# Second layer's latents: the spread of the keys' root and the key scale's product move inside the second query latent's section

## The chip, the cores and the metric

The kernel runs on one core of a Trainium2 chip. The time is device time in microseconds, the median of several executions. Lower is better. Five queues work at once on the core: PE (TensorE, matmuls and transposes, its weight loads shown apart as PEld), DVE (VectorE), ACT (ScalarE), POOL (GpSimd, which here mostly issues DMAs) and SP (SyncE, DMAs only). Each takes its instructions in the order in which the program was written, and waits on semaphores for the others.

## The reference

A two-layer encoder trunk: sequence 1024, width 1024, all in float32. Each layer has a mixer (latent attention beside a convolution branch) and a gated feed-forward part. The change is in the mixer's projections, of which this is what matters:

```python
h = _rmsnorm(x, g_mix[l])
p = h @ w_in[l]
c_q = _rmsnorm(p[..., :384], g_q[l])                  # query latent, 3 blocks of 128 channels
q = (c_q @ w_uq[l]).reshape(b, s, 8, 64 + 32)
c_kv = _rmsnorm(p[..., 384:640], g_kv[l])             # key/value latent, 2 blocks of 128
kv = (c_kv @ w_ukv[l]).reshape(b, s, 8, 64 + 64)      # k_nope and v
k_rope = _apply_rope(p[..., 640:672], cos, sin)
...                                                   # softmax attention over 8 heads
u = a * jax.nn.sigmoid(gt)                            # a, gt: the other 1024 columns of p
u = _dwconv(u, w_dw_conv[l], b_dw_conv[l])            # 31 taps along the sequence
```

## The kernel before

Activations lie transposed: 128 channels on the partitions, the 1024 tokens along the free dimension. A projection of 128 output channels is one **section** of PE work. A float32 product is made of three products of split operands (high and low parts, names ending in `h` and `l`), so a section of the second layer has 8 blocks of input channels x 3 products x 2 halves of 512 tokens = 48 matmuls.

The method `project` writes one layer's sections in a fixed order (`seq`). The part of the second layer that matters is: `kv0`, `kv1` (key/value latents), `kr` (the shared rotary key), `q0`, `q1`, `q2` (query latents), then `k0` to `k3` (keys, from the normalised `kv` latents), `u0`, `u1` (rotary parts of the queries) and `n0` to `n3` (the rest of the queries), both from the query latents. After each section's matmuls the loop calls `work`, which writes out what other engines have to do by then: each piece of follow-up work is a generator whose steps give an estimate of DVE time and of a delay, and `work` takes whichever step is due by a modelled clock, filling with convolution taps (`conv`, DVE) where nothing is due. So DVE and ACT instructions stand in the order in which `work`, `emit`, `after` and `evict` wrote them, and nothing is reordered when it runs.

What follows a latent section: ACT copies it out of PSUM (`cq<-pq`), squares it (`qss<-cq`), and makes its high part (`cqs_0h`), DVE the low part (`cqs_0l`) and the sum of squares. The keys' norm works like this:

- After `q0`'s matmuls PE transposes the summed squares (`rkv1t`), DVE reduces them and takes the root (`rkv1v`, `rkv1q`, `rkv1y`, function `roots`).
- `keys_norm`: PE spreads the root over the partitions by 8 transposes (`rkv1s`, function `spread`), ACT copies the two halves into `rkv`, DVE multiplies both latents by it (`ckv<-ckv,rkv`), ACT makes `kvs_0h` and `kvs_1h`, DVE `kvs_0l` and `kvs_1l`. The `k` sections read these four.
- `key_scale`: one small PE product (`kt`) sums numbers over the partitions, seven small DVE instructions make a power of two from it (`qk`), and the rotary key is split with it (`krs`, ACT then DVE).

PSUM in this stage: three full-width buffers (two banks each), taken in turn by the sections, and two single banks, taken in turn by `rkv1t`, `rkv1s` and `kt`. With the turn shift that stands before `q2`, `k0` takes the buffer of `q1`, `k2` that of `q2`, `k3` that of `k0`, `u0` that of `k1`. A `k` section's buffer comes free when DVE has made the low part of `ks` from it, after ACT has made the high part. `kt` takes the bank of the first half of `rkv1s`, so it waits for ACT's first copy into `rkv`.

Beside this ACT does work for later: `far` (a tap of the convolution scaled on ACT and added by an accumulating DMA that POOL issues), `wor` (sums of squares of the output weights), and `wu21l`, `wu01l`, `wu11l` (the negated high parts of weights; the load of the high part, `wu11h` and so on, is a DMA that POOL issues, in POOL's order behind the DMAs of the `far` tiles).

After `k3`, PE transposes the sum of the queries' squares (`rq1t`), `u0` runs, and PE spreads the queries' root (`rq1s`) between `u0` and `u1`; from there on the rest of the queries hangs.

Of the kernel before, what the change touches and what calls it, by code (L numbers as in the profile page):

```python
# [95 lines left out]
HALVES = (slice(0, 512), slice(512, T))  # L96
# [50 lines left out]
class Encoder:  # L147
# [102 lines left out]
                                           op0=ALU.mult, op1=ALU.subtract)  # L250
        return hi, lo

    def product(self, ps, weights, moving, by_half=False):
        nc = self.nc
        n = len(moving)
        for halves in ((0,), (1,)) if by_half else ((0, 1),):
            for k in range(n):
                (wh, wl), (xh, xl) = weights(k), moving[k]
                rest = ((wl, xh), (wh, xl)) if n <= 3 else ((wh, xl), (wl, xh))
                for s, (w, x) in enumerate(((wh, xh), *rest)):  # L260
                    for c in halves:
                        nc.tensor.matmul(ps[:, HALVES[c]], w, x[:, HALVES[c]], start=(k == 0 and s == 0),  # L262
                                         stop=(k == n - 1 and s == 2))
# [324 lines left out]
    def project(self, l, carry):  # L588
        nc, a = self.nc, self.a
        par = self.par[l]  # L590
        clock = {"pe": 0.0, "dve": 0.0}
        taps, active, u, conv, away, far_at = [], [], {}, {}, {}, {}
        gates, ckv, kvs, cq, cqs, vs, w = {}, [], [], [], [], [], {}
# [29 lines left out]
        def key_scale():  # L623
            sums = self.bank(f"kt{l}", (128, 3))
            nc.tensor.matmul(sums, self.ones, col(4, 3), start=True, stop=True)
            nc.vector.tensor_copy(out=col(4, 3), in_=sums)
            nc.vector.scalar_tensor_tensor(out=col(4), in0=col(4), scalar=float(KVL), in1=col(5), op0=ALU.mult, op1=ALU.mult)
            nc.vector.tensor_tensor(out=col(4), in0=col(4), in1=col(6), op=ALU.add)
            self.half_exponent(col(5), col(4))
            self.power(col(6), col(5), -1.0, 200.0)  # L630
            self.power(col(2), col(5), 1.0, 54.0)
            nc.vector.tensor_scalar(out=col(2), in0=col(2), scalar1=SCALE, scalar2=None, op0=ALU.mult)
            launch(key_rope_end())

        def work(until):
            while True:
                at = next((e for e in active if e[0] <= clock["dve"]), None)
                if at is None and taps and clock["dve"] + TAP <= until:
                    j, t = taps.pop(0)
                    self.conv_step(l, j, u[j], conv[j], t)  # L640
                    clock["dve"] += TAP
                    continue
                if at is None:
                    at = min(active, key=lambda e: e[0], default=None)
                    if at is None or at[0] > until:
                        return
                    clock["dve"] = max(clock["dve"], at[0])
                step = next(at[1], None)
                if step is None:
                    active.remove(at)  # L650
                else:
                    clock["dve"] += step[0]
                    at[0] = clock["dve"] + step[1]

        def launch(steps, n=-1):
            active.append([clock["pe"], steps, n])
# [5 lines left out]
                    e[0] = clock["dve"] + step[1]  # L662
                active.remove(e)

        def start(steps):
            next(steps)
            active.append([clock["pe"] + 1.8, steps, 99])

        def gate(j):
            g = gates[j] = self.blk(f"gate{l}_{j}")  # L670
# [52 lines left out]

        def keys_norm():
            r = st["rkv"] = self.blk(f"rkv{l}")
            for s, p in zip(HALVES, self.spread(rooted("kroot"), f"rkv{l}", HALVES, self.bank)):
                nc.scalar.copy(out=r[:, s], in_=p)
            yield 0.0, 1.8
            for j in range(2):
                nc.vector.tensor_tensor(out=ckv[j], in0=ckv[j], in1=r, op=ALU.mult)  # L730
                yield 1.25, 0.0
            both = [parts(ckv[j], f"kvs{l}_{j}", kvs, par[:, P_GKV + j:P_GKV + j + 1]) for j in range(2)]
            yield [next(p) for p in both][0]
            for p in both:
                yield from p
# [34 lines left out]
        def key_rope_end():  # L770
            t, hl = st.pop("kr"), self.blk(f"krs{l}", F16, (128, 2, T))[0:32]
            by = qk[0:32, 6:7]
            nc.scalar.activation(out=hl[:, 0], in_=t, func=AF.Copy, scale=by)
            yield 0.0, 1.5
            nc.vector.scalar_tensor_tensor(out=hl[:, 1], in0=t, scalar=by, in1=hl[:, 0], op0=ALU.mult, op1=ALU.subtract)
            self.move(krd, hl)
            yield 1.25, 0.0

        def query_latent(j):
            yield from latent(f"q{j}", cq, "qss", j)  # L780
            yield from parts(cq[j], f"cqs{l}_{j}", cqs, par[:, P_GQ + j:P_GQ + j + 1])

        def parts(src, name, out, scale):
            hi, lo = self.blk(name + "h", F32R), self.blk(name + "l", F32R)
            nc.scalar.activation(out=hi, in_=src, func=AF.Copy, scale=scale)
            yield 0.0, 1.5
            nc.vector.scalar_tensor_tensor(out=lo, in0=src, scalar=scale, in1=hi.bitcast(F32),
                                           op0=ALU.mult, op1=ALU.subtract)
            out.append((hi, lo))
            yield 1.25, 0.0  # L790
# [61 lines left out]

        def inputs(name):
            if l:
                return lambda: self.product(ps[name], lambda k: (w[name][:, 0, k], w[name][:, 1, k]), hl)
            return lambda: self.product(ps[name], self.tiled(w[name]), hl)

        def ranked(group, j, n, name, moving):
# [15 lines left out]
        def rooted(out):  # L874
            e = pending.pop(out)
            if e in active:
                for step in e[1]:
                    clock["dve"] = max(clock["dve"], e[0]) + step[0]
                active.remove(e)
            return st.pop(out)  # L880

        seq = []
        add = lambda name, weight, emit, evict, after=None: seq.append((name, weight, emit, evict, after))
# [10 lines left out]
            add(f"kv{j}", f"kv{j}", inputs(f"kv{j}"), lambda j=j: latent(f"kv{j}", ckv, "kss", j))  # L894
        add("kr", "kr", shared_key, key_rope)
        add("q0", "q0", inputs("q0"), lambda: query_latent(0), lambda: root("kss", "kroot", KVL, "rkv"))
        add("q1", "q1", inputs("q1"), lambda: query_latent(1), lambda: (start(keys_norm()), key_scale()))
        add("q2", "q2", inputs("q2"), lambda: query_latent(2))
        between = {2 + l: lambda: root("qss", "qroot", QL, "rq")}
        norm = lambda: start(queries_norm())  # L900
# [36 lines left out]
        hl, rx, ps = self.first_sections(l, supply) if l == 0 else self.next_sections(l, carry, supply)  # L937
# [295 lines left out]
    def up_steps(self, l, steps, put):  # L1233
# [238 lines left out]
        for q, (i, f) in enumerate(seq):  # L1472
            n = base + q
            steps.append(lambda i=i, f=f: product(i, f))
            m = EVICT.get((i, f), n + 1)
            put(int(m), m % 1 * 10, lambda i=i, f=f: evict(i, f))
# [844 lines left out]
```

## Time and profile before

| | |
|---|---|
| runs | 2175.66 us median of 3 (2175.47 to 2175.92) |
| profiled execution | 2174.71 us, of which the instructions' span is 2172.9 us |
| PE busy | 2160.1 us, 99% of the span |
| DVE, ACT, POOL busy | 1859.4 us (86%), 1480.1 us (68%), 517.2 us (24%) |
| granted TensorE clock, mean | 0.999 of 2.4 GHz |

The busy shares are means over the whole kernel. PE's share leaves 12.8 us of the span in which it isn't busy; whether an edit can win or lose time is seen from where PE waits, and for whom.

### The profile page before, as it was taken

Reading aid. Unit: us, or ns where it says so; the run is one execution under the profiler, and the core shown is the slowest. Engines: PE = TensorE matmul, PEld = TensorE weight load, DVE = VectorE, ACT = ScalarE, POOL = GpSimd, SP = SyncE. Lnnn points to the kernel's source line nnn. Section 1 sums busy time; section 2 is a strip of 40 time slices with the busy share of each in tenths; the row PEclk is TensorE's granted clock in tenths of the full one; section 3 lists DMA queues with packets and bytes.
Section 4 is the critical chain, followed back from the end, with each engine's and each line's share of the span. In section 5 each row is a group of like instructions: output and inputs, shape, how many; then the busy total and the mean of one; then the engine's idle time right before and its main releaser. Section 6 shows DMA issues by size and latency. Waiting matters only on the chain.

```text
span 2172.9 us, 29815 instructions
## 1 busy us (share of the span) xinstructions
PE 2160.1 (99%) x10726; PEld 1178.3 (54%) x10726; DVE 1859.4 (86%) x2558; ACT 1480.1 (68%) x2208; POOL 517.2 (24%) x506
## 2 busy tenths in 40 slices
PE   9999999999999999999999999999999999999998
PEld 8887666754444444444444576667544444444445
DVE  6989999879998887887978889998898988878877
ACT  6365888746898889554533768886478888865544
POOL 1232767211211111000000356771111111110000
PEclk9999999999999999999999999999999999999999
DMA  6898878854689898555334986786646988856533
GB/s 193 180 192 209 169 147 167 257 150 117 140 238 260 225 286 264 191 173 186 115 121 101 201 209 137 157 196 192 174 102 161 264 242 242 238 140 218 191 114 121
DMA packets 161220, 400.95 MB, mean 185 GB/s; under 512 B 19840, under 2 KB 27888, under 8 KB 161072
## 3 DMA queue, kind: packets, MB, share of 16 engines
q1 hardware_dynamic: 104080, 266.79, 35.8%
q0 software_dynamic: 56704, 131.74, 33.7%
q8 instruction: 84, 1.38, 0.3%
q10 hardware_dynamic: 288, 0.53, 0.1%
q14 instruction: 64, 0.52, 0.1%
HBM read 270.75 MB, written 69.66 MB: 157 GB/s over the span
## 4 chain that ended last, share of the span: by engine, by line
PE 93%; DVE 3%; ACT 2%; DMA 1%; issue 1%; DVEq 0%; SPq 0%; ACTq 0%
PE p L1376 36%; PE pd L1650 18%; PE po L1082 7%; PE s L1935 7%; PE t L1975 5%; PE pa L262 3%; PE o L1997 2%; PE pg L262 2%; PE pn L262 2%; PE pq L262 2%; PE pkv L262 1%; PE o L2002 1%; PE pg L585 1%; PE pv L1911 1%; PE pk L262 1%; DVE conv L2156 1%
## 5 line engine op out<-in xcount | busy, mean ns | idle before, releaser
L1376 PE MATMUL p<-b,w 128*128 128x512 f16 x3696 | 800.3, 379 | 0.3
L1376 PEld LDWEIGHTS <-w 128*128 128x128 f16 x3696 | 358.8, 98 | 431.7 <-issue 1.0
L1650 PE MATMUL pd<-ab,wd 128*128 128x512 f16 (+1 forms) x1920 | 401.0, 371 | 0.4 <-DVE ab L1640 0.4
L1252 POOL DMA_DIRECT2D wu<-in_w_up x176 | 152.5, 880 | 770.3 <-DVE w L1340 582.2
L1650 PEld LDWEIGHTS <-wd 128*128 128x128 f16 x1920 | 187.9, 98 | 210.7 <-issue 0.9
L1935 PE MATMUL s<-k,q 96*128 96x512 f16 x768 | 186.9, 379 | 0.0
L1340 DVE SCALAR_TENSOR_TENSOR w<-wu,wf,w 128x512 f16<-128x512 f32 (+1 forms) x216 | 177.3, 835 | 5.7 <-ACT w L1337 5.7
L1978 DVE SCALAR_TENSOR_TENSOR pt<-t,pt 128x512 f16<-128x512 f32 x256 | 163.0, 677 | 10.0 <-ACT pt L1977 9.0
L1337 ACT ACTIVATE w<-wu,wf 128x512 f16<-128x512 f32 (+1 forms) x216 | 165.2, 783 | 0.4 <-DMA wu<-in_w_up 0.4
L1977 ACT ACTIVATE pt<-t 128x512 f16<-128x512 f32 x256 | 139.2, 596 | 32.0 <-PE t L1975 30.0
L1937 DVE TENSOR_REDUCE mx<-s 128x1 f32<-128x1024 f32 x128 | 155.0, 1211 | 1.0 <-PE s L1935 1.0
L1639 ACT ACTIVATE ab<-ac,ds 128x512 f16<-128x512 f32 x108 | 75.6, 718 | 110.6 <-DVE ac L1545 73.6
L1945 ACT ACTIVATE p<-s,mx 128x1024 f32<-128x1024 f32 x128 | 143.3, 1120 | 2.3 <-DVE mx L1937 1.8
L2173 POOL TENSOR_SCALAR late<-gate,par 128x1012 f32<-128x1012 f32 (+14 forms) x99 | 135.8, 1372 | 27.4 <-PE pn L262 27.4
L2156 DVE SCALAR_TENSOR_TENSOR conv<-gate,par,conv 128x1009 f32<-128x1009 f32 (+14 forms) x110 | 139.7, 1274 | 2.8 <-ACT conv L688 0.2
L1975 PE MATMUL t<-ident,p 128*128 128x128 f32 x1024 | 136.6, 275 | 0.9 <-ACT p L1945 0.6
L1975 PEld LDWEIGHTS t<-ident,p 128*128 128x128 f32 x1024 | 116.8, 141 | 34.9 <-issue 8.2
L1883 DVE SCALAR_TENSOR_TENSOR o<-zg,par,o 128x1023 f32<-128x1023 f32 x88 | 112.8, 1282 | 10.0 <-ACT o L1877 8.4
L1883 DVE SCALAR_TENSOR_TENSOR v<-zv,par,v 128x1023 f32<-128x1023 f32 x88 | 112.2, 1277 | 1.4 <-ACT v L1877 1.4
L1384 DVE SCALAR_TENSOR_TENSOR zg<-p,wf,zg 128x512 f32<-128x512 f32 x72 | 54.0, 750 | 66.3 <-PE p L1376 52.7
L2163 POOL DMA_DIRECT2D conv<-far x31 | 26.5, 867 | 351.2 <-ACT far L2162 332.2
L1935 PEld LDWEIGHTS <-q 96*128 96x128 f16 x768 | 74.1, 97 | 64.5 <-issue 2.1
(1536 smaller groups left out, 3710.9 us busy)
## 6 DMA issues: line engine op xcount, KB each, us to landing
wu<-in_w_up SPq DMA_DIRECT2D x98, 512.0 KB
wu<-in_w_up POOLq DMA_DIRECT2D x176, 256.0 KB, 5.1
sd<-in_w_down SPq DMA_DIRECT2D x44, 512.0 KB
ws<-sd SPq DMA_DIRECT2D x44, 512.0 KB
act<-v SPq DMA_DIRECT2D x36, 512.0 KB
ac<-act SPq DMA_DIRECT2D x72, 256.0 KB
wo<-in_w_o POOLq DMA_DIRECT2D x32, 256.0 KB, 7.9
x_mix<-y SPq DMA_DIRECT2D x32, 256.0 KB
```

What stands on the lines that cost most here:

```text
L262: nc.tensor.matmul(ps[:, HALVES[c]], w, x[:, HALVES[c]], start=(k == 0 and s == 0), stop=(k == n - 1 and s == 2))
L1252: nc.gpsimd.dma_start(out=dst, in_=src, accum_op=ALU.add)
L1337: nc.scalar.activation(out=t, in_=src, func=AF.Copy, scale=scale[f])
L1340: nc.vector.scalar_tensor_tensor(out=t, in0=src, scalar=scale[f], in1=hi, op0=ALU.mult, op1=ALU.subtract)
L1376: nc.tensor.matmul(ps, w[p][:, k * 128:(k + 1) * 128], b[:, q], start=(i in (1, 5, 2) and k == 0 and t == 0), stop=(k == 3 and t == 2), sk ...
L1650: nc.tensor.matmul(ps[t, m][:, cs], w[i, j][p][:, m * 128:(m + 1) * 128], b[:, q, cs], start=(i in (1, 5, 2) and j == 0 and s == 0), stop= ...
L1883: self.nc.vector.scalar_tensor_tensor(out=o[:, a:b], in0=z[:, at + a:at + b], scalar=self.par[l][:, tap:tap + 1], in1=o[:, a:b], op0=ALU.m ...
L1935: nc.tensor.matmul(ps[:, cs], q[0:96, i, qs], k[0:96, j, cs], start=(s == 0), stop=(s == 2))
L1937: nc.vector.tensor_reduce(out=mx, in_=ps, op=ALU.max, axis=AX.X, negate=True)
L1975: nc.tensor.transpose(tp[:, i, qi * 128:(qi + 1) * 128], st["p"][2 * qp + qi][:, kt * 128:(kt + 1) * 128], self.ident)
L1978: nc.vector.scalar_tensor_tensor(out=lo, in0=tp, scalar=P_SCALE, in1=hi, op0=ALU.mult, op1=ALU.subtract)
L2156: self.nc.vector.scalar_tensor_tensor(out=y[:, lo:hi], in0=u[:, lo + s:hi + s], scalar=self.tap(l, j, t), in1=y[:, lo:hi], op0=ALU.mult, o ...
```

## The change

Only the second layer changes. `product` takes a table of functions to call ahead of given blocks of input channels. In `q1`'s section, ahead of block 4 (after 24 of its 48 matmuls) `keys_norm` is started, so the 8 transposes of `rkv1s` stand there; ahead of block 7 (after 42) `key_scale` is started, so `kt` stands there. Before, both stood behind `q1`'s last matmul. What follows them on ACT and DVE (the copies into `rkv` too, and the seven instructions on `qk`) is now written by `work`, from 5.8 and 9.6 us of its modelled clock past the start of the section.

```diff
-    def product(self, ps, weights, moving, by_half=False):
+    def product(self, ps, weights, moving, by_half=False, between={}):
         ...
             for k in range(n):
+                if k in between:
+                    between[k]()
...
         def key_scale():
             sums = self.bank(f"kt{l}", (128, 3))
             nc.tensor.matmul(sums, self.ones, col(4, 3), start=True, stop=True)
+            yield 0.0, 0.0
...
             launch(key_rope_end())
+            yield 1.2, 0.0
...
-        def start(steps):
+        def start(steps, wait=1.8):
             next(steps)
-            active.append([clock["pe"] + 1.8, steps, 99])
+            active.append([clock["pe"] + wait, steps, 99])
...
         def keys_norm():
             r = st["rkv"] = self.blk(f"rkv{l}")
-            for s, p in zip(HALVES, self.spread(rooted("kroot"), f"rkv{l}", HALVES, self.bank)):
+            spread = self.spread(rooted("kroot"), f"rkv{l}", HALVES, self.bank)
+            if l:
+                yield 0.0, 0.0
+            for s, p in zip(HALVES, spread):
                 nc.scalar.copy(out=r[:, s], in_=p)
...
             if l:
-                return lambda: self.product(ps[name], lambda k: (w[name][:, 0, k], w[name][:, 1, k]), hl)
+                between = {4: lambda: start(keys_norm(), 5.8), 7: lambda: start(key_scale(), 9.6)} if name == "q1" else {}
+                return lambda: self.product(ps[name], lambda k: (w[name][:, 0, k], w[name][:, 1, k]), hl, between=between)
...
-        add("q1", "q1", inputs("q1"), lambda: query_latent(1), lambda: (start(keys_norm()), key_scale()))
+        add("q1", "q1", inputs("q1"), lambda: query_latent(1), None if l else lambda: (start(keys_norm()), list(key_scale())))
```

The instructions are the same ones before and after; on PE, ACT and DVE some stand elsewhere, and POOL's and SP's rows keep their order. On PE, at the end of `q1`'s section (`pq_10693<-xs,wq1s`) and the start of `q2`'s (`wq2s`), this stands before:

```order
L262 MATMUL pq_10693<-xs_7_9795,wq1s 128x512
L339 MATMUL rkv1s<-ident,rkv1y 128x128 x8
L625 MATMUL kt_10785<-qk_9838,ones_r 128x3
L262 LDWEIGHTS wq2s
L262 MATMUL pq_10808<-xs_0_9697,wq2s 128x512
```

and this stands around `kt` in `q1`'s section now:

```order
L264 MATMUL pq_10693<-xs_6_9777,wq1s 128x512
L627 MATMUL kt_10760<-qk_9838,ones_r 128x3
L264 LDWEIGHTS wq1s
L264 MATMUL pq_10693<-xs_7_9795,wq1s 128x512
L264 LDWEIGHTS wq1s
L264 MATMUL pq_10693<-xs_7_9795,wq1s 128x512
```

`kt` moved from behind the section to ahead of its last six matmuls, and the transposes of `rkv1s` to the middle of it.

On ACT, from the high part of `q0`'s latent (`cqs_0h`) to that of `q1`'s (`cqs_1h`), before:

```order
L785 ACTIVATE cqs_0h<-cq_10679,par_155 128x1024
L727 COPY rkv_10772<-rkv1s 128x512 x2
L709 ACTIVATE cq_10794<-pq_10693,wz 128x1024
L719 ACTIVATE qss_1_10796<-cq_10794 128x1024
L225 ACTIVATE wu21l<-wu21h 128x768
L617 ACTIVATE wor_1b,sc_9839<-wor_1b 128x1024
L773 ACTIVATE krs_10804<-krt_10657,qk_9838 32x1024
L2162 ACTIVATE far_0_19_10857<-gate_0_10052,par_155 128x1020
L2162 ACTIVATE far_1_19_10860<-gate_1_10114,par_155 128x1020
L2162 ACTIVATE far_2_19_10863<-gate_2_10257,par_155 128x1020
L785 ACTIVATE kvs_0h<-ckv_10467,par_155 128x1024
L785 ACTIVATE kvs_1h<-ckv_10541,par_155 128x1024
```

and now:

```order
L792 ACTIVATE cqs_0h<-cq_10679,par_155 128x1024
L734 COPY rkv_10718<-rkv1s 128x512 x2
L792 ACTIVATE kvs_0h<-ckv_10467,par_155 128x1024
L792 ACTIVATE kvs_1h<-ckv_10541,par_155 128x1024
L780 ACTIVATE krs_10801<-krt_10657,qk_9838 32x1024
L713 ACTIVATE cq_10803<-pq_10693,wz 128x1024
L723 ACTIVATE qss_1_10805<-cq_10803 128x1024
L225 ACTIVATE wu21l<-wu21h 128x768
L619 ACTIVATE wor_1b,sc_9839<-wor_1b 128x1024
L2170 ACTIVATE far_0_19_10864<-gate_0_10052,par_155 128x1020
L2170 ACTIVATE far_1_19_10867<-gate_1_10114,par_155 128x1020
L2170 ACTIVATE far_2_19_10870<-gate_2_10257,par_155 128x1020
```

`kvs_0h`, `kvs_1h` and `krs` moved up to stand right behind the copies; everything ahead of the copies, and everything behind `cqs_1h`, keeps its place.

On DVE, from `q0`'s low part (`cqs_0l`) to that of the first key latent (`kvs_0l`), without the seven small rows on `qk` but the first, before:

```order
L787 SCALAR_TENSOR_TENSOR cqs_0l<-cq_10679,par_155,cqs_0h 128x1024
L2156 SCALAR_TENSOR_TENSOR conv_3_10459<-gate_3_10389,par_155,conv_3_10459 128x1018
L2156 SCALAR_TENSOR_TENSOR conv_3_10459<-gate_3_10389,par_155,conv_3_10459 128x1019
L2156 SCALAR_TENSOR_TENSOR conv_3_10459<-gate_3_10389,par_155,conv_3_10459 128x1020
L626 COPY qk_9838<-kt_10785 128x3
...
L775 SCALAR_TENSOR_TENSOR krs_10804<-krt_10657,qk_9838,krs_10804 32x1024
L730 TENSOR_TENSOR ckv_10467<-ckv_10467,rkv_10772 128x1024
L730 TENSOR_TENSOR ckv_10541<-ckv_10541,rkv_10772 128x1024
L280 SCALAR_TENSOR_TENSOR qss_10681<-qss_10681,qss_1_10796 128x1024
L2156 SCALAR_TENSOR_TENSOR conv_3_10459<-gate_3_10389,par_155,conv_3_10459 128x1021
L787 SCALAR_TENSOR_TENSOR kvs_0l<-ckv_10467,par_155,kvs_0h 128x1024
```

and now:

```order
L794 SCALAR_TENSOR_TENSOR cqs_0l<-cq_10679,par_155,cqs_0h 128x1024
L2164 SCALAR_TENSOR_TENSOR conv_3_10459<-gate_3_10389,par_155,conv_3_10459 128x1019
L629 COPY qk_9838<-kt_10760 128x3
...
L737 TENSOR_TENSOR ckv_10467<-ckv_10467,rkv_10718 128x1024
L737 TENSOR_TENSOR ckv_10541<-ckv_10541,rkv_10718 128x1024
L782 SCALAR_TENSOR_TENSOR krs_10801<-krt_10657,qk_9838,krs_10801 32x1024
L794 SCALAR_TENSOR_TENSOR kvs_0l<-ckv_10467,par_155,kvs_0h 128x1024
```

One tap went ahead of `cqs_0l`, one behind the key latents, and `krs` behind the two products. Farther down, one more tap (`128x1022`) moved from ahead of the `ks` rows to between `ks_2` and `ks_3`.

## Rows read from the trace of the kernel before

**Rows 1.** The page's first part: busy time of PE, share of span, instructions.

```profile
PE 2160.1 (99%) x10726; PEld 1178.3 (54%) x10726; DVE 1859.4 (86%) x2558; ACT 1480.1 (68%) x2208; POOL 517.2 (24%) x506
```

**Rows 2.** Windows: us, busy (instructions) by engine, granted clock, DMA share, GB/s.

```profile
1232.00:1236.00 4.00, 2.17 (x9) 1.11 (x8) 4.00 (x5) 3.97 (x5) 1.46 (x2) 1.00 1.09 216
...
1277.00:1467.00 190.00, 189.57 (x1163) 115.91 (x1162) 172.50 (x226) 157.85 (x286) 137.27 (x113) 1.00 0.80 174
```

**Rows 3.** PE's timeline: start, length, instructions [idle before <-who ended it].

```profile
1209.41 10.52 PE L262 MATMUL pq<-xs,wq1s 128*128 128x512 f16 x48
1219.77 1.04 PE L339 MATMUL rkv1s<-ident,rkv1y 128*128 128x128 f32 x8
1221.83 0.38 PE L625 MATMUL kt<-qk,ones_r 128*128 128x3 f32 x2 [1.03 <-ACT rkv L727]
1222.08 10.52 PE L262 MATMUL pq<-xs,wq2s 128*128 128x512 f16 x48
...
1235.62 0.73 PE L262 MATMUL pk<-kvs_0l,wk1h 128*128 128x512 f32 x2 [1.76 <-DVE kvs_0l L787]
...
1245.72 1.03 PE L301 MATMUL rq1t<-ident,qss 128*128 128x128 f32 x8
...
1251.11 1.06 PE L339 MATMUL rq1s<-ident,rq1y 128*128 128x128 f32 x8 [0.26 <-DVE rq1y L317]
```

**Rows 4.** ACT's timeline in the same stretch, same columns.

```profile
1221.22 1.04 ACT L727 COPY rkv<-rkv1s 128x512 f32<-128x512 f32 x2
1222.16 1.11 ACT L709 ACTIVATE cq<-pq,wz 128x1024 f32<-128x1024 f32 x1
...
1227.32 1.15 ACT L773 ACTIVATE krs<-krt,qk 32x1024 f16<-32x1024 f32 x1 [1.19 <-DVE qk L983]
1228.38 3.20 ACT L2162 ACTIVATE far<-gate,par 128x1020 f32<-128x1020 f32 x3
...
1239.51 1.09 ACT L797 ACTIVATE ks<-pk,qk 128x1024 f16<-128x1024 f32 x1
...
1242.15 0.85 ACT L225 ACTIVATE wu11l<-wu11h 128x768 fp32r<-128x768 f32 x1 [0.51 <-DMA wu11h<-in_w_uq]
1242.91 2.10 ACT L797 ACTIVATE ks<-pk,qk 128x1024 f16<-128x1024 f32 x2
```

**Rows 5.** DVE's timeline in the same stretch, same columns.

```profile
1214.36 0.17 DVE L317 SCALAR_TENSOR_TENSOR rkv1y<-rkv1q,rkv1y 128x8 f32<-128x8 f32 x1
1221.35 1.28 DVE L787 SCALAR_TENSOR_TENSOR cqs_0l<-cq,par,cqs_0h 128x1024 fp32r<-128x1024 f32 x1 [6.82 <-ACT cqs_0h L785]
1222.55 3.91 DVE L2156 SCALAR_TENSOR_TENSOR conv<-gate,par,conv 128x1018 f32<-128x1018 f32 x3
1226.37 0.15 DVE L626 COPY qk<-kt 128x3 f32<-128x3 f32 x1
...
1229.70 2.34 DVE L730 TENSOR_TENSOR ckv<-ckv,rkv 128x1024 f32<-128x1024 f32 x2
...
1240.64 1.28 DVE L799 SCALAR_TENSOR_TENSOR ks<-pk,qk,ks 128x1024 f16<-128x1024 f32 x1 [1.48 <-ACT ks L797]
...
1244.16 2.47 DVE L799 SCALAR_TENSOR_TENSOR ks<-pk,qk,ks 128x1024 f16<-128x1024 f32 x2
1247.07 1.28 DVE L799 SCALAR_TENSOR_TENSOR ks<-pk,qk,ks 128x1024 f16<-128x1024 f32 x1 [0.43 <-ACT ks L797]
1248.27 1.28 DVE L312 TENSOR_REDUCE rq1v<-rq1t 128x4 f32<-128x512 f32 x2
```

**Rows 6.** POOL's timeline: the DMAs of three far tiles, then the load.

```profile
1229.81 0.88 POOL L2163 DMA_DIRECT2D conv<-far  x1 [3.21 <-ACT far L2162]
...
1232.41 1.05 POOL L210 DMA_DIRECT2D wu11h<-in_w_uq  x1
```

**Rows 7.** DMA issues between 1195 and 1275 us: KB, us from issue to landing.

```profile
wu01h<-in_w_uq POOLq DMA_DIRECT2D x1, 384.0 KB, 9.0
...
wu11h<-in_w_uq POOLq DMA_DIRECT2D x1, 384.0 KB, 9.7
```

## The prediction

> **What bounds the kernel now.** I read the page's busy shares first: PE is busy 99% of the span [rows 1], so the end moves only by what PE waits. Then PE's timeline from `q1` to `u1` in the second layer, where its waits stand in brackets: 1.03 us ahead of `kt`, for ACT's first copy into `rkv`; 1.76 us inside `k0`, for DVE's `kvs_0l`; 0.26 us ahead of `rq1s`, for the queries' root [rows 3]. Together 3.05 us, 0.14% of the time, and that is all that this stretch can give back. Behind it PE is busy 189.57 of 190 us [rows 2]: what `rq1s` gains or loses reaches the end one for one. Last I read ACT and DVE in the same stretch, since they are waited for [rows 4, 5]. There the reader is to see that ACT hardly rests: from 1222.16, behind the copies, to the high part of `ks_0` at 1239.51, its one wait is 1.19 us. And the copies themselves start at 1221.22, though PE had ended the transposes at 1219.77 + 1.04 = 1220.81 [rows 3]: ACT's own queue sets them.
>
> **The change part by part.** *The spread.* `q1`'s matmuls stand (1219.77 - 1209.41) / 48 = 0.216 us apart [rows 3]; 24 of them end at 1214.6. The root is there at 1214.36 + 0.17 = 1214.53 [rows 5], and a tap of 1.2 us earlier now, because the reduction moves ahead of it. So the eight transposes find their input, and cost what they cost before, some 1.0 us.
>
> *The product `kt`.* PE comes to it after 42 matmuls and the transposes, at 1209.41 + 9.07 + 1.0 = 1219.5. Its bank is that of the first half of `rkv1s`, so it waits for ACT's first copy. Every ACT row ahead of the copies is where it was, so the copy is not earlier, and `kt` starts at 1221.83 as before. The wait of 1.03 us becomes one of 2.3, and behind it on PE now stand the six last matmuls of `q1`, 1.3 us: `q2` starts at 1223.4 instead of 1222.08, `k0` at 1223.4 + 10.4 = 1233.8.
>
> *DVE.* `cqs_0l` still waits for ACT until 1221.35; one tap stands behind it, where there were three, so the first `qk` row comes at 1222.55 + 1.20 = 1223.75 instead of 1226.37 [rows 5]. The `qk` rows took 0.95 us until they released `krs` [rows 4, 5] and have one more of some 0.15 behind; `ckv` starts at 1224.9, and the two products end at 1226.1 and 1227.25 (2.34 us both). Behind them DVE waits for ACT's `krs`, third in ACT's row from 1226.15 at steps of 1.05 and 1.15 us long: 1229.5. Then `krs`, `kvs_0l`, `kvs_1l` at 1.2 us each: the last ends at 1233.2, ahead of `k0`. So the wait of 1.76 us goes. The 44 `k` matmuls from 1235.62 to 1245.72 are 0.23 us apart; 48 from 1233.8 end at 1244.8. If nothing else were late, `rq1t` would come 0.9 us earlier.
>
> *What it costs on ACT.* Before, the copies were followed by other work while DVE made `ckv`. Now `kvs_0h` stands right behind the copies and waits for `ckv`, from about 1222.2 to 1226.15, with everything behind it. Between the copies and `ks_0` the same instructions stand as before, 1239.51 - 1222.16 - 1.19 = 16.16 us of work. They start at 1226.15, `kvs_1h` waits another 0.1 for the second product, so the high part of `ks_0` starts at 1242.4, 2.9 us late. `q1`'s copy (`cq`) is among the delayed, at 1229.4, but `k0` needs its buffer only at 1233.8; `q2`'s copy, at 1237.5 to 1238.6, still precedes `k2` at 1239.3.
>
> *What PE then waits for.* `k3` needs `k0`'s buffer. The low part of `ks_0` runs on DVE from 1242.4 + 1.09 = 1243.5 to 1244.8; PE would be there at 1233.8 + 36 x 0.23 = 1242.1 and waits 2.7 us. `k3` ends at 1247.5. `rq1s` needs the queries' root, which stands on DVE behind all four `ks` rows. Before, from `ks_0` (1240.64) to the reduction `rq1v` (1248.27) DVE worked 7.63 - 0.43 us; now one more tap is among them, 1.2, so at least 8.4 us: `rq1v` at 1251.9, and `rq1s` 2.84 later as before [rows 3, 5], 1254.7. That is 3.6 us later than 1251.11, whatever else happens: the lower bound of the loss.
>
> *What the DMAs add.* Between `ks_0` and `ks_1` ACT has `wu11l`, which reads the load `wu11h`. Before, ACT was there at 1242.15 - 0.51 = 1241.6 and waited 0.51 us for it [rows 4]. POOL issues the load behind the DMAs of three `far` tiles [rows 6], and ACT makes these tiles later: they lose the 2.9 us and also the place of `kvs_0h` and `kvs_1h`, which stood behind them (2.06 us at 1.03). The `far` row moves from 1228.38 to 1233.3, the issue of `wu11h` from 1232.41 to 1237.3. It took 9.7 us to land, and its like behind the three earlier `far` DMAs 9.0 [rows 7]: 1246.3 to 1247.0. ACT is there at 1244.4 and stands. From the first `far` DMA's issue the load landed 12.3 us later (1229.81 to 1242.15), which with 1234.7 gives 1247.0; I take 1246.8. From there: `wu11l` to `ks_1` 0.76, its high part 1.10, then on DVE from `ks_1` to `rq1v` 4.11 - 0.43 as before and the tap, 4.9, then 2.84: 9.6 us. `rq1s` at 1256.4, which is 5.3 us late. `u0` (4.1 us, from `ks_1`'s low part at 1250.0) ends ahead of that. The landing decides from 1254.7 - 9.6 = 1245.1 on; each microsecond later costs one. Bounds of this term: nothing (3.6 in all) to a landing 1.3 us past the rows' 1247.0 (6.8), since the queue could also be emptied slower than in these two cases. I choose near the rows because the pattern, three accumulations and a load, is the same.
>
> The Trainium skill, "DMA: Bandwidth & Descriptors", section on the anatomy of one DMA on the SWDGE (gpsimd) path, fits such a DMA by 2.0 us and its bytes at 436 GB/s; for 384 KB that is an estimate of 2.9 us, by which the load would land at 1240.2 and the sum would be the lower bound, +3.6. The trace disagrees: 9.7 and 9.0 us, with the queue full of `far` DMAs.
>
> Everything behind `rq1s` keeps its order, and its inputs come from PE or were shifted by at most as much, so nothing gives the time back. Other moves cost nothing: the taps end in the same stretch, `krs` leaves DVE at about 1230.7, a microsecond later, for a DMA that is read only in the attention; POOL's other loads have 7 us and more until the `n` sections.
>
> **The sum.** The profiled execution took 2174.71 us: a span of 2172.9 and 1.8 around it. With 5.3 it is 2180.0. The runs' median is 0.95 us above that execution, so the forecast is 2175.66 + 5.3 = **2181.0 us**, 0.24% slower. About 0.2%, 4.35 us, is what a measurement of this kernel can tell from no change; so the forecast lies only just beyond it.
>
> **The rivals.**
> - *The load is no limit.* With fewer DMAs beside it `wu11h` lands before 1245.1, 7.8 us after its issue, and the loss is the lower bound: 2175.66 + 3.6 = 2179.3. For it: the landing times are those of a full queue, and ACT's delay spreads the issues. Against it: the three `far` DMAs right ahead are what fills it, and they move along. The skill's fit above speaks for this case. Chance 0.23.
> - *ACT's lateness does not reach PE* (the other side). If ACT had room, so that `ks_0` came by 1240 as before, PE would keep the gain of the removed wait: `rq1t` 0.9 us earlier, 2174.7. It decides at `k3`: the low part of `ks_0` must end by 1242.1, 2.7 us earlier than I have it. It would take copies into `rkv` some 3 us earlier, or `ckv` ready behind them. The 99% of PE and the removed wait speak for it, the order of ACT's rows against it. Chance 0.07. Even with all 3.05 us gone the time would be 2172.6, within 0.2%: a gain that can be measured is nearly excluded, 0.02.
> - *The clock.* PE is thin from 1242 to 1256, with waits of 2.7, 1.7 and 2.3 us. If the granted clock fell to 1.2 GHz there, `u1`'s 4.1 us would double: 5.3 + 4.1, 2185.1. Against it: where PE was busy 2.17 of 4 us the granted clock stayed 1.00 [rows 2]. Chance 0.06. The Trainium skill, "TensorE: Matmul & The Clock Gate", Part 1, says that the throttled clock is the default and activity releases it; no run here shows how little is enough.
>
> **How the numbers follow.** The forecast with landings from 1246.0 on has 0.62: 4.5 to 6.8 us, slower. The first two rivals have 0.30, within 0.2%; the clock 0.06, slower; faster 0.02. So slower 0.67, same 0.31 (a part of the forecast's lower end is within 0.2%), faster 0.02. The range goes from just under the lower bound of the loss, 2178.9, to the late landing, 2182.6; it leaves out the second rival and the clock.
>
> **What the profile after would show.** PE: `kt` inside `q1`, waiting some 2.3 us for ACT `rkv`; no wait for `kvs_0l`; new waits of about 2.7 us at `k3` for DVE `ks`, of about 1.7 at `u0` and of 2.3 at `rq1s`. ACT: a wait of some 4 us at `kvs_0h` for DVE `ckv`, and one of about 2.4 at `wu11l` for the DMA. If ACT's wait at `kvs_0h` is short, step four is wrong and with it the sign; if it is there and `wu11l` doesn't wait, only the size is.

## The result, and the profile after

The changed kernel takes 2180.07 us (median of 11 runs, 2179.51 to 2181.80), the kernel before in the same comparison 2175.47 us (11 runs, 2173.74 to 2175.92): a ratio of 1.0024, 95% interval 1.0015 to 1.0034. It is slower, since the interval lies above 1; whether by more than the 0.2% that the prediction took as its limit isn't settled, since the interval begins below that. The forecast was 2181.0 us in a range of 2178.9 to 2182.6.

The profiled execution took 2181.61 us, its span is 2179.8 us, and PE is still busy for 99% of it. PE's timeline of the same stretch as in [rows 3], of the kernel after: start, length, instructions, and in brackets the wait ahead of them and who ended it.

```profile
1208.89 5.34 PE L264 MATMUL pq<-xs,wq1s 128*128 128x512 f16 x24
1214.07 1.04 PE L341 MATMUL rkv1s<-ident,rkv1y 128*128 128x128 f32 x8
...
1221.30 0.38 PE L627 MATMUL kt<-qk,ones_r 128*128 128x3 f32 x2 [2.31 <-ACT rkv L734]
1221.55 1.83 PE L264 MATMUL pq<-xs,wq1s 128*128 128x512 f16 x6
1223.16 11.88 PE L264 MATMUL pq<-xs,wq2s 128*128 128x512 f16 x48
...
1244.20 0.73 PE L264 MATMUL pk<-kvs_0h,wk1h 128*128 128x512 f32 x2 [0.98 <-DVE ks L806]
...
1247.06 1.03 PE L303 MATMUL rq1t<-ident,qss 128*128 128x128 f32 x8
1250.16 0.73 PE L264 MATMUL pu<-cqs_0h,wu21h 128*128 128x512 f32 x2 [2.06 <-DVE ks L806]
...
1256.43 1.76 PE L341 MATMUL rq1s<-ident,rq1y 128*128 128x128 f32 x8 [1.89 <-DVE rq1y L319]
```

The wait for `kvs_0l` (1.76 us) is gone; `kt` waits 2.31 us instead of 1.03, and three waits are new: 0.98 us at `k3`, 2.06 at `u0`, and 1.89 instead of 0.26 at `rq1s`. Where `q1` starts differs by up to a microsecond between profiles (1209.41 before, 1208.89 here), so I count from `q1`'s start: `rq1s` came 1251.11 - 1209.41 = 41.70 us behind it, and comes 47.54 us behind it now, 5.84 us later.

ACT's timeline shows where it comes from:

```profile
1220.69 1.04 ACT L734 COPY rkv<-rkv1s 128x512 f32<-128x512 f32 x2
1225.54 1.15 ACT L792 ACTIVATE kvs_0h<-ckv,par 128x1024 fp32r<-128x1024 f32 x1 [3.81 <-DVE ckv L737]
...
1232.68 3.21 ACT L2170 ACTIVATE far<-gate,par 128x1020 f32<-128x1020 f32 x3
...
1241.73 1.09 ACT L804 ACTIVATE ks<-pk,qk 128x1024 f16<-128x1024 f32 x1
...
1246.94 0.84 ACT L225 ACTIVATE wu11l<-wu11h 128x768 fp32r<-128x768 f32 x1 [3.08 <-DMA wu11h<-in_w_uq]
1247.69 3.11 ACT L804 ACTIVATE ks<-pk,qk 128x1024 f16<-128x1024 f32 x3
```

Right behind the copies ACT stands 3.81 us for `ckv`. Before, `kvs_0h` stood behind the `far` tiles and waited for nothing:

```profile
1231.49 1.13 ACT L785 ACTIVATE kvs_0h<-ckv,par 128x1024 fp32r<-128x1024 f32 x1
```

Now everything behind it is late: the `far` tiles, and with them the load of `wu11h`, for which ACT stands another 3.08 us; so the last three `ks` follow one another only from 1247.69 on. DVE in the same stretch is the one that ACT waits for, and then waits for ACT in its turn (4.24 us):

```profile
1220.81 1.28 DVE L794 SCALAR_TENSOR_TENSOR cqs_0l<-cq,par,cqs_0h 128x1024 fp32r<-128x1024 f32 x1 [5.50 <-ACT cqs_0h L792]
...
1224.29 2.35 DVE L737 TENSOR_TENSOR ckv<-ckv,rkv 128x1024 f32<-128x1024 f32 x2
...
1242.86 1.28 DVE L806 SCALAR_TENSOR_TENSOR ks<-pk,qk,ks 128x1024 f16<-128x1024 f32 x1 [4.24 <-ACT ks L804]
...
1248.82 2.48 DVE L806 SCALAR_TENSOR_TENSOR ks<-pk,qk,ks 128x1024 f16<-128x1024 f32 x2 [2.35 <-ACT ks L804]
1251.21 1.28 DVE L2164 SCALAR_TENSOR_TENSOR conv<-gate,par,conv 128x1022 f32<-128x1022 f32 x1
1252.40 1.28 DVE L806 SCALAR_TENSOR_TENSOR ks<-pk,qk,ks 128x1024 f16<-128x1024 f32 x1
```

A part of the loss is DVE's own: the tap that the change put between `ks_2` and `ks_3` holds up `ks_3`, and with it the queries' root, by 1.19 us (1252.40 - 1251.21), since ACT's last `ks` row was done at 1250.80 (1247.69 + 3.11). The prediction counted 1.2 for it; no run takes this tap alone away.

POOL's timeline gives the issue of the load:

```profile
1236.71 1.05 POOL L210 DMA_DIRECT2D wu11h<-in_w_uq  x1
```

and the list of DMA issues its landing (KB, us from the issue):

```profile
wu11h<-in_w_uq POOLq DMA_DIRECT2D x1, 384.0 KB, 10.2
```

Last the windows, with the granted clock behind POOL's column. In the first profile of the kernel before, the clock was 1.00 in the whole stretch. Now it fell to 0.50, that is 1.2 GHz, twice: behind `kt`'s wait and around `rq1s` and `u1`.

```profile
1223.00:1225.00 2.00, 2.00 (x6) 0.73 (x5) 1.83 (x9) 0.00 (x0) 0.00 (x0) 0.50 1.08 212
...
1257.00:1260.00 3.00, 3.00 (x11) 2.61 (x10) 1.04 (x1) 2.32 (x3) 0.00 (x0) 0.50 0.40 160
```

### The profile page after: what moved, and what is told of

Its sections match the earlier page's. It is cut to its first block, busy times and chain, and to the rows that moved or that the text cites. A ratio compares the mean times of both kernels' runs of the same rounds, so it can differ in the third digit from the quotient of the medians.

```text
span 2179.8 us, 29815 instructions
## 1 busy us (share of the span) xinstructions
PE 2162.9 (99%) x10726; PEld 1179.4 (54%) x10726; DVE 1859.4 (85%) x2558; ACT 1478.8 (68%) x2208; POOL 516.5 (24%) x506
## 4 chain that ended last, share of the span: by engine, by line
PE 94%; ACT 3%; DVE 2%; issue 1%; DMA 0%; SPq 0%; DVEq 0%; ACTq 0%
PE p L1384 36%; PE pd L1658 18%; PE po L1090 7%; PE s L1943 7%; PE t L1983 5%; PE pa L264 3%; PE o L2005 2%; PE pg L264 2%; PE pg L587 2%; PE pn L264 2%; PE pq L264 2%; PE pkv L264 1%; PE o L2010 1%; PE pv L1919 1%; PE pa L587 1%; DVE conv L2164 1%
```

## The experiments

The theory: the loss is ACT's. `kvs_0h` stands behind the copies and waits for `ckv`; `ks`, and by way of the `far` tiles the load, come late, and through them `rq1s`. Its rival: the loss is PE's own, the longer wait of `kt` with six matmuls of `q1` behind it, and the clock that falls there. A second rival puts it on the falls of the clock alone. Beside all of them stands the tap ahead of `ks_3`, shown above.

All kernels in one measure, from one profile each; "late" is how much farther behind `q1`'s start `rq1s` stands than 41.70 us, "rest" what the span has behind `rq1s`. Medians and ratios are of the timed runs, 8 to 11 of a kernel, with the 95% interval. Each ratio is to runs of the kernel before in the same comparison; their medians were 2175.47 us for the changed kernel, 2174.11 for e1 to e4, 2174.95 for e5 to e8 and 2174.44 for e9 and e10, so a ratio can't be had from the first row of the table. They differ with the share of runs in the upper of the two groups into which the times of the kernel before fall (7 of 11, 11 of 30, 15 of 31 and 9 of 21; see e11 and e12).

| kernel | median us | ratio to before | late us | rest us |
|---|---|---|---|---|
| before | 2175.47 | | 0 | 921.8 |
| after | 2180.07 | 1.0024 [1.0015, 1.0034] | 5.84 | 923.4 |
| e1 PE's order alone | 2175.86 | 1.0007 [0.9998, 1.0016] | 2.15 | 921.7 |
| e2 ACT's order alone | 2179.83 | 1.0025 [1.0015, 1.0036] | 5.85 | 921.8 |
| e3 `wu11l` later | 2177.33 | 1.0013 [1.0005, 1.0022] | 3.41 | 921.8 |
| e4 copies earlier | 2178.47 | 1.0018 [1.0009, 1.0027] | 4.37 | 921.8 |
| e5 after, again | 2179.86 | 1.0025 [1.0015, 1.0035] | 5.66 | 921.8 |
| e6 root's spread alone | 2177.52 | 1.0013 [1.0004, 1.0022] | 3.39 | 921.8 |
| e7 `ckv` first | 2177.49 | 1.0013 [1.0005, 1.0022] | 3.24 | 921.8 |
| e8 and less ahead of `ks` | 2174.95 | 1.0002 [0.9993, 1.0011] | 0.60 | 922.2 |
| e9 and ACT without gaps | 2174.28 | 0.9996 [0.9987, 1.0005] | -0.97 | 922.2 |
| e10 before, less ahead of `ks` | 2175.38 | 1.0001 [0.9992, 1.0010] | 0.00 | 921.8 |
| e11 before, again | 2175.73 (one) | | 1.63 | 921.7 |
| e12 before, again | 2173.86 (one) | | 0.01 | 921.8 |

Behind `rq1s` three rows differ by more than 0.1 us: after, by 1.6 (the clock, see e5), e8 and e9, by 0.4, which no run explains. The rest of the effect lies between `q1` and `rq1s`.

**e1, PE's order alone.** `rkv1s` and `kt` stand inside `q1` as in the changed kernel; what follows them on ACT and DVE is written behind `q1`.

```diff
-between = {4: lambda: start(keys_norm(), 5.8), 7: lambda: start(key_scale(), 9.6)} if name == "q1" else {}
+between = {4: lambda: early(keys_norm()), 7: lambda: early(key_scale())} if name == "q1" else {}
...
-None if l else lambda: (start(keys_norm()), list(key_scale()))
+rest if l else lambda: (start(keys_norm()), list(key_scale()))
```

> PE's order is that of the changed kernel (the transposes of rkv1s after 24 of q1's matmuls, kt after 42), but everything on ACT and DVE that follows them is written behind q1, as before the change. My theory (the loss is ACT standing at kvs_0h for DVE's ckv): kt waits about 2.3 us inside q1 for ACT's rkv copy, ACT has no long wait for ckv, a short wait for kvs_0l at k0 takes most of what kt lost, rq1s comes 0 to 0.9 us later than in the kernel before: 2175.5 to 2176.5 us. Rival (the wait of kt inside q1, 1.3 us more than before, and the clock behind it, 1.4 us of matmuls at half speed, is what the change costs): 2178 to 2180 us.

**e2, ACT's order alone.** The kernel before, with the first four steps of `keys_norm` written at once, so that `kvs_0h` and `kvs_1h` stand behind the copies.

```diff
-lambda: (start(keys_norm()), key_scale()))
+lambda: (start_far(keys_norm()) if l else start(keys_norm()), key_scale()))
```

> PE's order is that of the kernel before (rkv1s and kt behind q1), but kvs_0h and kvs_1h are written right behind the copies into rkv on ACT, as in the changed kernel. My theory: ACT stands at kvs_0h for DVE's ckv 4 to 5.5 us, ks_0 comes 3 us or more late, the load of wu11h some 5 us late, rq1s 5 to 6 us late: 2180.5 to 2181.5 us, the whole loss though nothing moved on PE. Rival (the wait of kt inside q1 is the cost): 2175.5 us, as before.

PE's timeline in e1:

```profile
1221.83 0.38 PE L627 MATMUL kt<-qk,ones_r 128*128 128x3 f32 x2 [2.31 <-ACT rkv L743]
1222.08 2.71 PE L264 MATMUL pq<-xs,wq1s 128*128 128x512 f16 x6
...
1237.05 0.73 PE L264 MATMUL pk<-kvs_0l,wk1h 128*128 128x512 f32 x2 [0.54 <-DVE kvs_0l L803]
```

`kt` waits its 2.31 us, and the clock falls behind it (six matmuls take 2.71 us, in e3 behind the same wait 1.46). `q1` ends later for both, ACT's copy of `q1` waits for that, and `kvs_0l` comes 1.43 us later than in [rows 3], although `q1` had started at the same time. `rq1s` is 2.15 us late, more than my 0 to 0.9, though the median, 2175.86 us, lies in the range I gave. So PE's part is not nothing; taken alone it is about a third of the loss in this profile, the fall of the clock included, and the runs can't tell e1 from the kernel before (interval 0.9998 to 1.0016). In e2, with PE in its old order, the loss is all there. ACT's timeline in e2, and PE's:

```profile
1226.66 1.15 ACT L790 ACTIVATE kvs_0h<-ckv,par 128x1024 fp32r<-128x1024 f32 x1 [5.37 <-DVE ckv L735]
```

```profile
1236.46 0.85 PE L262 MATMUL pk<-kvs_0l,wk1h 128*128 128x512 f32 x2 [3.90 <-DVE kvs_0l L792]
...
1250.93 0.73 PE L262 MATMUL pu<-cqs_0h,wu21h 128*128 128x512 f32 x2 [1.71 <-DVE ks L804]
```

So the theory stands: ACT's order makes a loss of this size without PE's, and PE's doesn't make it without ACT's. That 5.85 is so near 5.84 is chance. In e2 DVE has three taps ahead of `ckv` and not one, so ACT's wait is 5.37 and not 3.81, and PE waits for `kvs_0l` instead of at `k3`; on the other side no tap stands between `ks_2` and `ks_3`. The median, 2179.83 us, is below the 2180.5 to 2181.5 expected: those were counted from the upper of the two groups of the kernel before. And the two parts don't add up in the changed kernel (2.15 + 5.85 is more than 5.84): there PE's delay in `q1` goes into the wait at `k3` (see e5).

**e3, the load's part.** `wu11l` stands behind the `ks` rows.

```diff
-while turning and turning[0][1] <= now + turn:
+while turning and turning[0][1] <= now + (9.0 if l and turning[0][0] == "u1" else turn):
```

> The changed kernel, but the negated high part wu11l stands on ACT behind the ks rows, so that no ks waits for the load wu11h. My theory: the lower bound of the loss is left, rq1s 3.6 us later than before the change: 2179.1 us, and 1.5 to 2.2 us less than the changed kernel in executions of like clock, with no wait of ACT for a DMA ahead of ks_1. Rival (the load is hidden and the loss is all DVE's later ks_0): the changed kernel's 2180.1 us. Rival (the load's landing is most of the loss): 2176 to 2177 us.

PE's timeline in e3:

```profile
1221.32 1.46 PE L264 MATMUL pq<-xs,wq1s 128*128 128x512 f16 x6
...
1243.97 1.22 PE L264 MATMUL pk<-kvs_0h,wk1h 128*128 128x512 f32 x2 [2.63 <-DVE ks L806]
```

`rq1s` is 3.41 us late against 3.6: the lower bound of the prediction, measured. The load's part is 5.84 - 3.41 = 2.4 us, or 2.3 against e5; the prediction had 1.7. The time expected, 2179.1, was counted from the upper group of the kernel before (see e11); 2177.33 was measured.

**e4, the copies earlier.** They are written with the spread, ahead of the `far` tiles on ACT.

```diff
 spread = self.spread(rooted("kroot"), f"rkv{l}", HALVES, self.bank)
-if l:
-    yield 0.0, 0.0
 for s, p in zip(HALVES, spread):
```

> The changed kernel, but the two copies into rkv are written right behind the spread, so ahead of the far tiles that stand before them on ACT. My theory: kt no longer waits in q1 (under 0.5 us), yet ACT still waits some 2.5 us at kvs_0h, since DVE has cqs_0l ahead of ckv; most of the loss stays: rq1s 3 to 4.5 us late, 2178.5 to 2180 us. Rival (the wait of kt is the cost): the whole loss goes, 2172.5 to 2175.5 us.

ACT's timeline in e4:

```profile
1223.85 1.15 ACT L790 ACTIVATE kvs_0h<-ckv,par 128x1024 fp32r<-128x1024 f32 x1 [2.55 <-DVE ckv L735]
```

and PE's:

```profile
1218.38 0.28 PE L627 MATMUL kt<-qk,ones_r 128*128 128x3 f32 x2
...
1243.50 1.22 PE L264 MATMUL pk<-kvs_0h,wk1h 128*128 128x512 f32 x2 [4.25 <-DVE ks L804]
```

`kt` waits for nothing, and still 4.37 us of the loss are there. PE is early and gives it back at `k3`, where it waits 4.25 us. ACT's wait of 2.55 is the number expected, from DVE's order alone.

**e5, after again**, unchanged, for a second profile.

> The changed kernel once more, for a second profile. Counted from the start of q1, rq1s came 5.8 us late in its first profile, and the granted clock was 0.50 twice, behind kt's wait and again at rq1s and u1. My theory: ACT's wait at kvs_0h (3.8 us), DVE's late ks and ACT's wait for wu11h (about 3 us) are there again and rq1s is 5.3 to 5.9 us late; the second fall of the clock, which cost 1.6 us, need not be there, and without it the rest behind rq1s takes 921.8 us, as in the kernel before. Rival (the clock's falls are the loss): in a profile without them rq1s is under 4 us late.

PE at `k3` in e5, and the window of e5 that answers to the second fall:

```profile
1243.93 0.74 PE L264 MATMUL pk<-kvs_0h,wk1h 128*128 128x512 f32 x2 [0.94 <-DVE ks L806]
```

```profile
1257.00:1260.00 3.00, 3.00 (x15) 2.48 (x14) 2.06 (x2) 1.96 (x3) 0.53 (x1) 1.00 0.44 178
```

The second fall isn't there, the rest takes 921.8 us and not 923.4, and `rq1s` is as late as before (5.66). So the second fall isn't the loss; it cost 1.6 us in the first profile, whose span is 2 us longer than that of this one. The first fall is in e5 too (0.50 behind `kt`'s wait), and it isn't the loss either: `k3` starts 35.31 us behind `q1` in after, in e5, and in e3, where that fall is missing. PE waits there for `ks_0`, and a delay of `q1` and `q2` only shortens the wait (0.98, 0.94 and 2.63 us).

**e6, the root's spread alone.** `key_scale` stands behind `q1` as before the change, `keys_norm` inside it.

```diff
-between = {4: lambda: start(keys_norm(), 5.8), 7: lambda: start(key_scale(), 9.6)} if name == "q1" else {}
+between = {4: lambda: start(keys_norm(), 5.8)} if name == "q1" else {}
...
-None if l else lambda: (start(keys_norm()), list(key_scale()))
+(lambda: list(key_scale())) if l else lambda: (start(keys_norm()), list(key_scale()))
```

> Half of the change: keys_norm starts inside q1's section as in the changed kernel, but key_scale, kt and all, stands behind q1's last matmul as before. So PE's wait for ACT's rkv copy is as in the kernel before (about 1.0 us), and kvs_0h still stands right behind the copies on ACT. My theory: ACT waits 2.5 to 3 us at kvs_0h for ckv, krs on ACT comes late and brings back a wait of 1 to 2 us for kvs_0l, the load wu11h comes late, rq1s is 3.3 to 5 us later than in the kernel before, counted from q1: 3.3 to 5 us slower. Rival (kt's place in q1 is what costs): within 1 us of the kernel before.

PE's waits in e6 (us in total, times, longest):

```profile
PE pk L264 <- DVE ks L806: 2.4, 1, 2.4
PE pk L264 <- DVE kvs_0l L794: 1.3, 1, 1.3
PE kt L627 <- ACT rkv L734: 1.0, 1, 1.0
```

`rq1s` is 3.39 us late, as expected, with `kt`'s wait at its old length. The wait for `kvs_0l` is back because `krs` is late on ACT: DVE's `krs`, which stands ahead of `kvs_0l`, waits 5.09 us for it.

**e7 to e9, the same move on PE with ACT's queue cleared step by step.** e7: copies with the spread, `ckv` ahead of `cqs_0l` on DVE, `wu11l` late. e8: moreover the squares of `wor_2b` and `wor_3b` behind the copies into `rq`, and no tap from `k2` to `u1`. e9: moreover `kvs_0h`, `kvs_1h` and `krs` behind `q1`'s copy and square, `wu21l` and `wor_1b`.

```diff
-between = {4: lambda: start(keys_norm(), 5.8), 7: lambda: start(key_scale(), 9.6)} if name == "q1" else {}
+between = {4: lambda: start(keys_norm(), 3.0), 7: lambda: start(key_scale(), 9.6)} if name == "q1" else {}
...
-            out_squares(clock["pe"])
+            if not (l and name in ("k0", "k1", "k2", "k3", "u0")):
+                out_squares(clock["pe"])
+            st["hold"] = l and name in ("k2", "k3", "u0", "u1")
```

These are the edits of e7 (beside those of e3 and e4) and of e8, where `work` writes no tap while `hold` is set. In e9, `keys_norm` and `key_scale` pause ahead of `kvs_0h` and `krs` (for which `key_scale` starts with 90.0 instead of 9.6), and go on when the loop has come to `q2`'s section:

```diff
-                yield 1.25, 0.0
+                yield 1.25, 90.0 if l and j else 0.0
...
+            if l and name == "q2":
+                for e in [e for e in active if e[2] == 99]:
+                    step = next(e[1])
+                    clock["dve"] += step[0]
+                    e[0] = clock["dve"] + step[1]
```

> The changed kernel with both copies into rkv written right behind the spread, DVE's two products ckv ahead of cqs_0l instead of behind it, and wu11l behind the ks rows on ACT. My theory: ACT no longer waits for ckv at kvs_0h (under 0.3 us), kt does not wait, nothing waits for wu11h; ACT has about 1.5 us at krs for qk, PE waits about 3 us at k3 for ks_0, rq1s is 0.5 to 1.5 us later than in the kernel before, counted from q1: so 4 to 5 us less than the changed kernel. Rival (something else in the change costs, for instance the transposes inside q1 or the tap ahead of ks_3 alone): 3 us or more later than the kernel before.

> The last kernel, and two more things taken from ahead of the ks rows: the squares of wor_2b and wor_3b on ACT stand behind the copies into rq (2.1 us less ahead of ks_0), and the tap between ks_2 and ks_3 on DVE stands behind u1's section (1.2 us less ahead of the queries' root). My theory: the queue in front of the ks rows sets rq1s, so it now comes 1.5 to 2.5 us earlier than in the kernel before, counted from q1: 2172 to 2173.5 us, the first of these kernels below the kernel before. Rival (the waits of PE are set elsewhere): as the last kernel, 0.5 to 1.5 us above the kernel before.

> The kernel of e8, but on ACT kvs_0h and kvs_1h no longer stand right behind cqs_0h: q1's copy and square (cq, qss), wu21l and the square of wor_1b stand ahead of them, then the two, then krs and the far tiles. In e8, ACT stood 1.4 us at krs for qk and 3.0 us at cq and qss for the DMAs that read older far tiles, and PE waited 2.2 us for cq at k2. My theory (ACT's queue in front of the ks rows sets the time): at least 2 of these 4.4 us are filled with work, ks_0 comes 2 to 3.4 us earlier than in e8, and rq1s 1 to 2.8 us earlier than in the kernel before, counted from q1: 1 to 2.4 us less than the kernel before. Rival (the DMAs of the far tiles set it, whatever stands where): rq1s within 0.5 us of e8's, which is 0.6 us later than in the kernel before.

e7 came out 3.24 us late instead of 0.5 to 1.5, the number of its rival (3 us or more, something else in the change costs). Nothing waits for `ckv` any more, but ACT's list of waits has something new:

```profile
ACT qss L723 <- DMA conv<-far: 1.5, 1, 1.5
ACT krs L778 <- DVE qk L989: 1.4, 1, 1.4
...
ACT cq L713 <- DMA conv<-far: 0.8, 1, 0.8
```

`kvs_0h`, `kvs_1h` and `krs` were given their buffers ahead of `cq` and `qss`, so these two got the buffers that accumulating DMAs of older `far` tiles were still reading. Moving an instruction up moves its buffer too. The buffers come from one pool, in the order in which the program asks for them; the changed kernel asks in the same order, but its ACT comes to `cq` only at 1228.82 and waits for no DMA there. What part of the 3.24 us these waits make isn't measured alone. e8 has the same waits (0.4 and 2.6) and is 0.60 late, not 1.5 to 2.5 early, which is the number of its rival; its time is level with the kernel before. e9 has no such wait but 0.2 us at a `far` tile, and `rq1s` comes 0.97 us earlier than before, just short of the 1 to 2.8 expected and outside its rival (within 0.5 of e8). What holds it is on DVE: two taps stand between the high part of `ks_0`, done at 1237.1 (1236.00 + 1.09 on ACT), and its low part:

```profile
1237.22 2.59 DVE L2169 SCALAR_TENSOR_TENSOR conv<-gate,par,conv 128x1020 f32<-128x1020 f32 x2
1239.73 1.28 DVE L804 SCALAR_TENSOR_TENSOR ks<-pk,qk,ks 128x1024 f16<-128x1024 f32 x1
```

Its time can't be told from the kernel before (0.9996, interval 0.9987 to 1.0005). From e7 to e9 PE's own order is the same, and 4.2 us of lateness went by moving work on ACT and DVE (the tap between `ks_2` and `ks_3` among it).

**e10, the control for e8 and e9**: the kernel before, with their edits of `wu11l`, `wor` and the taps.

> The kernel before, with only those edits of e7 and e8 that are no part of the change: wu11l and the squares of wor_2b and wor_3b behind the copies into rq on ACT, no tap between k2's and u1's sections. Nothing of the change is in it. My theory: PE's waits of 1.0 us for kt and 1.8 us for kvs_0l stay, and PE itself, not the ks rows, sets rq1s: within 0.5 us of the kernel before. Rival (these edits, and not the moved spread, are what e8 and e9 live from): 1 us or more less than the kernel before.

`rq1s` is 0.00 us late: in the kernel before, these edits are worth nothing. `ks_0` comes earlier, but the last three `ks` rows on ACT then wait for PE's `k` sections (0.57, 1.60 and 1.61 us), so there PE sets `rq1s`.

**e11 and e12, before again**, unchanged.

> The kernel before, unchanged, for another profile. Its times fall into two groups, about 2173.9 and 2175.7 us, and so do those of e10, which has the same waits of PE; the kernels without the wait for kvs_0l don't show two groups so far apart. My theory: the upper group are executions in which the granted clock falls to half behind the wait for kvs_0l (1.76 us) in k0, as it did behind longer waits in other kernels; an execution of the upper group shows k0's matmuls twice as far apart for some 3 us and rq1s 1.3 to 1.9 us later, counted from q1. Rival (the stretch up to q1, or the rest behind rq1s, makes the difference): rq1s is 41.7 us behind q1's start in both groups.

> The same once more, since one profile falls into the upper group only about 4 times in 10. The same is expected: by my theory rq1s is 41.7 us behind q1's start in an execution near 2173.9 us and 43 us or more in one near 2175.7; by the rival 41.7 in both.

One execution of each group came. The same window behind the wait for `kvs_0l`, which is 1.76 us in both, of e11 (2175.73 us):

```profile
1236.00:1239.00 3.00, 3.00 (x9) 2.32 (x8) 2.67 (x3) 3.00 (x6) 1.20 (x1) 0.50 1.13 188
```

and of e12 (2173.86 us):

```profile
1236.00:1239.00 3.00, 3.00 (x15) 2.49 (x14) 2.38 (x2) 3.00 (x7) 1.20 (x1) 1.00 1.10 175
```

At half the clock 9 matmuls start instead of 15, and `rq1s` is 1.63 us later. So the kernel before has a cost that its first profile doesn't show: in some executions the clock falls behind its wait of 1.76 us, and that costs 1.6 us more. One profile shows it; that the other times near 2175.7 are of the same kind is inferred from the times. The changed kernel, which has no such wait, is 5.7 us above the lower group (2179.54 for e5's profiled execution against 2173.86 for e12) and 4.6 above the median of 11 runs, 7 of which were in the upper group.

## Why the prediction was right, step by step

- *The spread finds its input* and *the copies are not earlier*: so. `kt` waits 2.31 us (2.3 said), the wait for `kvs_0l` is gone.
- *ACT stands some 4 us at `kvs_0h`*: 3.81. From this step came the sign, and e2 shows that such a wait is enough by itself. `ks_0` started at 1241.73, which is 32.84 us behind `q1`; 1242.4 - 1209.41 = 32.99 was said.
- *The wait at `k3`*: 2.7 us said, 0.98 measured. The step took `q1`'s tail and `q2` at full clock. They took 1.83 and 11.88 us; in e3, without a fall of the clock at this place, 1.46 and 10.52, and there the wait at `k3` is 2.63 us. The 1.7 us that the clock took went out of the wait, and `rq1t` came when it was said: 38.17 us behind `q1`, 38.1 said. In e3 the clock fell behind this longer wait instead (0.50 from 1244 to 1247), and `rq1t` came 39.57 us behind `q1`. At `u0` PE waited 2.06 us (1.7 said), at `rq1s` 1.89 (2.3 said).
- *The load*: issued 27.82 us behind `q1` (27.9 said), but it took 10.2 us to land and not the 9.5 on which 1246.8 rests. So `wu11l` waits 3.08 us and not 2.4, and this term is 2.4 us (5.84 against e3's 3.41) where 1.7 was in the sum. The other term, the lower bound, is 3.4 (e3) where 3.6 was. In e2, e3 and e5 the load took 9.8 to 10.0 us. The Trainium skill, "DMA: Bandwidth & Descriptors", section on the anatomy of one DMA, has a fit that gives an estimate of 2.9 us for such a load. All of these, each behind three `far` DMAs of the same queue, took over three times that; no run shows this load without them.
- *The rest gives nothing back*: so, 921.8 us in e5. But the rival *the clock* (0.06) did come, in one of the two profiled executions and for 1.6 us instead of 4.1: it was 0.50 from 1257 to 1260 and 0.99 from 1260 to 1263, so only a part of `u1` was at half speed. What was said against it, that the clock stayed 1.00 where PE was busy 2.17 of 4 us, was read in a single execution: the wait in that window is the one for `kvs_0l`, behind which e11 shows 0.50.
- *The level.* The 5.3 us were worked out from a profile at full clock (2174.71 us) and added to a median (2175.66) whose three runs lie in the upper group, where by e11 a fall of the clock has its 1.6 us; the changed kernel doesn't have that wait. Against e12's 2173.86 us the level is 1.8 us too high. The lateness was put 0.4 to 0.5 us too low (5.3 for 5.66 to 5.84), and the second fall lengthens some executions of the changed kernel. So that the forecast missed 2180.07 by only 0.9 us is in part luck: errors of opposite sign. With like added to like, e12's 2173.86 and the measured lateness of 5.7 give 2179.5, and e5's execution, in which the second fall is missing, took 2179.54.
- *The load is no limit* (0.23): refuted by e3, where no `ks` waits for the load and 2.4 us are gained. *ACT's lateness doesn't reach PE* (0.07): it does, at `u0` and `rq1s`. What that rival asked for, copies 3 us earlier and `ckv` behind them, is e7 to e9; with ACT's queue cleared as well it gains 0.97 us.

## What to carry to other kernels

An instruction that is moved up in an in-order queue takes its wait with it: before moving one, look at who feeds it and what stands behind it, since `kvs_0h`, which had found its input ready in its old place, made ACT stand 3.81 us (5.37 in e2) in front of everything that it does next. It takes its buffer along as well, and whoever is pushed back in the rotation may get one that a DMA still reads (e7). And compare like with like: where a wait makes the clock fall in some executions only, one profile and a median can be of two different kinds, and an estimate from the one must not be added to the other.

## What the hardware showed that I had not expected

The granted clock falls behind waits as short as these, and not always. Behind the 1.76 us for `kvs_0l` it fell in e11 and not in e10, e12 or the first profile; behind `kt`'s 2.31 us it fell in after, e1 and e5 (to 0.50) and not in e3, where six matmuls took 1.46 us. In e8 and e9, with waits of 2.17 and 2.03 us in the `k` sections, it didn't fall in this stretch. In e11 it read 0.50 from 1236 to 1239 with PE busy 3.00 of 3.00 us; where no later wait covered that (around `rq1s` and `u1` in after, in `k0` in e11), it cost 1.6 us. The Trainium skill, "TensorE: Matmul & The Clock Gate", Part 1, has the throttled clock as the default that activity releases. These rows agree with it, in that the clock fell behind waits; that it fell behind the same wait in one execution and not in another is what the runs add.
